# First stage as a planned order of steps, and the last two dense blocks of a chunk interleaved by pairs of channel tiles

## The chip, the cores and the metric

The kernel runs on one core of one Trainium2 chip. The metric is the device time of one execution in microseconds (us). Five engines run side by side, each with its own queue of instructions, taken in order: TensorE (PE: matrix products; its weight loads are listed as PEld), VectorE (DVE), ScalarE (ACT), GpSimd (POOL) and SyncE (SP), which here does little but issue DMAs. An instruction that waits for another engine holds up all that stands behind it on its own engine.

## What is computed

One layer of a streaming encoder on 4096 tokens of width 1024, in float32. Cut to what matters here:

```python
h = rms_norm(x, norm_g[layer])
proj = h @ w_in[layer]                       # 1024 -> 4648 columns
q, k, v, qi, ki, wi, z_a, u_b, z_b, gates = jnp.split(proj, SPLIT_POINTS, axis=-1)
q = apply_partial_rope(rms_norm(q, q_norm_g[layer]), cos_a, sin_a)
k = apply_partial_rope(rms_norm(k, k_norm_g[layer]), cos_a, sin_a)
...                                          # qi, ki turned alike
iscore = jnp.einsum('bqhs,bqh->bqs', jax.nn.relu(logits), wib)
_, idx = lax.top_k(iscore, k_sel)            # 256 keys of each query
a = dsa_attention(q, k, v, qi, ki, wi, k_sel) * jax.nn.silu(z_a)
b = multiscale_pool(u_b, pool_w[layer], pool_scale[layer]) * jax.nn.silu(z_b)
g = jax.nn.sigmoid(gates.reshape(B, S, N_BRANCHES, D_MODEL) + merge_bias[layer])
y = g[:, :, 0] * (a @ w_branch_a[layer]) + g[:, :, 1] * (b @ w_branch_b[layer])
x = x + y @ w_out[layer]
```

## The kernel before

Products of float32 are made of three products of halves: every operand is split into a high part (rounded to the PE's input format, written by ACT) and a low part (the rest, a subtraction), and high x high, high x low and low x high are summed in PSUM (`mm3`, L342). The work has four stages, one behind the other.

**First stage (`phase1`, L351).** For each of 32 tiles of 128 tokens: load x, its mean square (`stats`, L382), scale it, turn it 128 x 128 on PE with the halves split out of PSUM (`transp`, L391, two times four turns), project it with 1064 columns of `w_in` in three groups, q (512 columns), kv (256) and i (296) (`project`, L407), and then `evac` (L417): norms and rotation of q and k on ACT, DVE and POOL, the halves written to DRAM. `index_key` (L470) turns the index key of a tile into the resident array `kis`. The halves of h go to DRAM too (`hD`), for the dense products of the second stage. The order of the instructions is the order in which the code is written: L497 to L568 give a start by hand, and a loop in which tile t is projected while tile t + 2 is turned and the statistics of tile t + 3 are made. In the start, tiles 0 and 1 are projected 256 columns at a time as the split weights come in (`weights`, L476, whose raw tiles have two buffers); the angle tables (`tables`, L285) are made ahead of that on DVE. A PSUM buffer `pt` (two of them) takes the turned x and also the turned index key.

**Second stage (`phase_index`, L660).** The search of the 256 keys runs beside the dense products of the columns that are left. The order is made by a planner (`Plan`, L146): each step has an engine, a cost, a key (about a due time) and the steps it waits for; `run` plays them in order of keys with these costs and calls each step's function when it starts, which writes the instruction. So the order of each engine is fixed when the kernel is built, from the planner's costs, and the chip's own times decide only how long the engines wait for each other. The search: scores on PE (`ps`, L767), Relu on ACT (L770), the weighted sum on DVE (L772) into `ring`; then seven rounds of counting per group of query tiles (ACT `sg`, L857, and the update of the bound on DVE, L816 to L845), the 256th value (L885 to L897, `flag`) and the bias rows (L905). A count of the flags (L935) is read by all engines before the third stage.

The dense products (`dense`, L941): six sweeps of four or five blocks of 128 columns; each sweep goes over eight chunks of 512 tokens, and for each chunk over its blocks, each of 24 products of 512 columns into a PSUM buffer `pd` (three of them). The halves of h come from DRAM as eight tiles `h` per chunk (pairs of channel tiles, high and low, 512 KB each) into a ring of 12. A block ends in a sigmoid on ACT (`sgm`, L969, L1004, L1011), which frees `pd` or lets DVE free it.

**Third and fourth stage**: attention over the chosen keys, and the output products. The change doesn't touch their code.

Of the kernel before, what the change touches and what calls it, by code (L numbers as in the profile page):

```python
# [24 lines left out]
NB = S // P  # L25
# [83 lines left out]
WSP = 10000.0  # L109
HLD = 40.0  # L110
# [24 lines left out]
class Plan:  # L135
# [43 lines left out]
    def run(self, lat):  # L179
# [12 lines left out]
        while left:  # L192
# [16 lines left out]
            if start:  # L209
# [8 lines left out]
                busy[s.eng] = now + s.cost + (CHF if form.get(s.eng, 0) != s.form else 0.0)  # L218
# [17 lines left out]
            else:  # L236
                assert nxt is not None, "the plan has no step to go on with"
                now = nxt
        return now
# [13 lines left out]
class K:  # L253
# [6 lines left out]
    def consts(self):  # L260
        nc, cp, a = self.nc, self.cp, self.a
# [5 lines left out]
        ii = c1.tile([P, P], I32, name="ii")  # L267
        nc.gpsimd.iota(ii, pattern=[[1, P]], base=0, channel_multiplier=-1)
        self.ident = ci.tile([P, P], F32, name="ident")
        nc.vector.tensor_scalar(self.ident, ii, 0.0, None, op0=OP.is_equal)  # L270
        self.identr = cp.tile([P, P], F32R, name="identr")
        nc.scalar.activation(self.identr, self.ident, AF.Copy)
        self.kis = ci.tile([P, S], F32R, name="kis")
        self.wi = ci.tile([P, NB, 8], F32, name="wi")
        self.qn2 = ci.tile([P, NB, 9], F32, name="qn2")
        self.k31 = ci.tile([P, P], F32R, name="k31")
# [4 lines left out]
        nc.scalar.dma_start(self.cst, a["cst"])  # L281
        nc.scalar.dma_start(self.col, a["col"])
        self.gqk = c1.tile([P, 10, 64], F32, name="gqk")

    def tables(self, rp):  # L285

        nc, a = self.nc, self.a
        with self.tc.tile_pool(name="prep", reuse_waits="tile", bufs=1) as sp:
            pos_i = sp.tile([P, NB], I32, name="pos_i")
            nc.scalar.dma_start(pos_i, a["pos"])  # L290
            gq = sp.tile([P, 2, 64], F32, name="gq")
            nc.scalar.dma_start(gq[:, 0], bass.AP(tensor=a["q_norm_g"].tensor, offset=a["q_norm_g"].offset,
                                                  ap=[[0, P], [1, 64]]))
            nc.scalar.dma_start(gq[:, 1], bass.AP(tensor=a["k_norm_g"].tensor, offset=a["k_norm_g"].offset,
                                                  ap=[[0, P], [1, 64]]))
            nc.vector.tensor_scalar(self.gqk[:, 0:8], bc(gq[:, 0:1], [P, 8, 64]), 0.125, None, op0=OP.mult)
            nc.vector.tensor_copy(self.gqk[:, 8:10], bc(gq[:, 1:2], [P, 2, 64]))
            pos = sp.tile([P, NB], F32, name="pos")
            nc.vector.tensor_copy(pos, pos_i)

            sh = [P, NB, 12]
# [10 lines left out]
            for piece in TWO_PI[:3]:  # L312
                for m in (nh, nl):
                    nc.vector.scalar_tensor_tensor(ang, m, -piece, ang, op0=OP.mult, op1=OP.add)
# [1770 lines left out]
```

## Time and profile before

| | us |
|---|---|
| time, median of 3 runs (4126.26 to 4133.24) | 4131.97 |
| the profiled execution, its own time | 4129.07 |
| its span, first to last instruction | 4127.3 |
| PE busy in the span | 3975.5 (96%) |
| DVE busy | 3239.9 (78%) |
| ACT busy | 2254.5 (55%) |
| POOL busy | 2012.3 (49%) |

A busy PE is not a PE at its peak: its products overlap, and a row's length is longer than the distance to the next row. So the text below goes by the distance from start to start. "Idle before" is the time that an engine stood still just ahead of an instruction, and the engine behind the arrow is the one that ended the wait. In a row of the timeline the columns are start, length, engine, line, operation, what is written `<-` what is read, and count. Where the trace gives a clock (PEclk), it is the share of full speed that was granted to TensorE.

### The profile page before, as it was taken

The page shows a single profiled execution, that of the slowest core. Times are in us where ns is not written, and L with a number is a line of the kernel's source. Part 1 is how long each engine was busy: PE and PEld are TensorE (multiplying, and loading weights), DVE is VectorE, ACT ScalarE, POOL GpSimd, SP SyncE. Part 2 cuts the span into 40 slices and gives each one's busy share as a digit, 9 for nine tenths or more (in the row PEclk, how much of TensorE's full clock was granted, in tenths as well). Part 3 has the DMA queues.
Part 4 walks back from the last instruction along what each step waited for, and adds up shares of the span by engine and source line. Part 5 has one row for each costly group of instructions (what it writes and reads, how often), then busy time and mean ns, then how long its engine had stood idle before and what let it go on. Part 6 is the DMA issues. An engine that isn't in the chain of part 4 may idle for free.

```text
span 4127.3 us, 63967 instructions
## 1 busy us (share of the span) xinstructions
PE 3975.5 (96%) x22940; PEld 3030.1 (73%) x22941; DVE 3239.9 (78%) x6389; ACT 2254.5 (55%) x3163; POOL 2012.3 (49%) x1623
## 2 busy tenths in 40 slices
PE   7999999999999999999979999999999999999999
PEld 6888888787777777788756666666666666887887
DVE  5555688888888888777679999999999995556654
ACT  4444687777777877877545555555554543111221
POOL 3555412213213223010028889999999994334653
PEclk9999999999999999999979999999999999999999
DMA  7766645544446446566563443332222215887543
GB/s 232 272 237 231 201 168 179 181 165 166 169 164 204 145 153 203 209 230 213 203 150 73 78 75 66 59 62 54 56 54 43 47 25 165 282 256 237 189 158 123
DMA packets 515986, 637.36 MB, mean 154 GB/s; under 512 B 230608, under 2 KB 365392, under 8 KB 511696
## 3 DMA queue, kind: packets, MB, share of 16 engines
q1 hardware_dynamic: 487632, 608.18, 46.7%
q10 hardware_dynamic: 28032, 25.06, 2.7%
q8 instruction: 181, 2.97, 0.3%
q14 instruction: 141, 1.16, 0.1%
HBM read 409.48 MB, written 191.76 MB: 146 GB/s over the span
## 4 chain that ended last, share of the span: by engine, by line
PE 60%; DVE 15%; issue 7%; ACT 5%; POOL 5%; DMA 5%; SPq 1%; ACTq 0%; DVEq 0%; POOLq 0%
PE pv L1550 8%; PE p L2003 7%; PE st L1498 7%; PE p L1854 7%; PE pd L1061 7%; PE pd L1060 7%; PE pd L1062 6%; PE ps L767 4%; DVE jk L1439 4%; PE ps L1430 3%; DVE ring L772 2%; ACT sg L857 2%; DMA h<-hD 2%; POOL row L431 2%; DVE tt L1511 1%
## 5 line engine op out<-in xcount | busy, mean ns | idle before, releaser
L1529 POOL TENSOR_TENSOR acc<-acc,tt 128x1024 f32<-128x1024 f32 x388 | 928.0, 2392 | 67.2 <-ACT tt L1510 40.4
L1510 ACT ACTIVATE tt<-tt 128x1024 f32<-128x1024 f32 (+1 forms) x544 | 560.9, 1034 | 553.0 <-DVE tt L1511 520.0
L1061 PE MATMUL pd<-h,wgh 128*128 128x512 f32 x1792 | 706.3, 394 | 9.0 <-DMA h<-hD 8.5
L1060 PE MATMUL pd<-h,wgh 128*128 128x512 f32 x1792 | 711.0, 397 | 0.3 <-DMA h<-hD 0.3
L772 DVE SCALAR_TENSOR_TENSOR ring<-rl,wi,ring 128x1024 f32<-128x1024 f32 (+7 forms) x624 | 698.2, 1165 | 11.3 <-ACT rl L770 8.0
L1062 PE MATMUL pd<-h,wgl 128*128 128x512 f32 x1792 | 705.7, 394 | 0.0
L770 ACT ACTIVATE rl<-ps 128x1024 f32<-128x1024 f32 (+7 forms) x624 | 536.2, 887 | 182.2 <-DVE ring L772 62.1
L1511 DVE TENSOR_TENSOR tt<-st,bT 128x1024 f32<-128x1024 f32 (+1 forms) x504 | 600.5, 1193 | 12.1 <-PE st L1498 11.9
L1550 PE MATMUL pv<-tt,vv 128*64 128x256 f32 x4224 | 518.9, 387 | 2.5 <-ACT ov L1571 1.9
L857 ACT ACTIVATE sg<-ring,tk 128x2048 fp8e4<-128x2048 f32 (+9 forms) x322 | 485.1, 1508 | 63.5 <-DVE tk L845 34.0
L1439 DVE CUSTOM_DVE_ANT_1 jk<-ps,bias,mf 128x1024 bf16<-128x1024 f32 (+3 forms) x408 | 469.4, 1151 | 19.5 <-PE ps L1430 17.5
L1550 PEld LDWEIGHTS pv<-tt,vv 128*64 128x64 f32 x4224 | 287.1, 138 | 171.6 <-issue 38.0
L1061 PEld LDWEIGHTS pd<-h,wgh 128*128 128x128 f32 x1792 | 338.1, 189 | 83.2 <-DMA h<-hD 15.5
L1062 PEld LDWEIGHTS pd<-h,wgl 128*128 128x128 f32 x1792 | 337.9, 189 | 75.5
L1060 PEld LDWEIGHTS pd<-h,wgh 128*128 128x128 f32 x1792 | 337.9, 189 | 74.4 <-DMA h<-hD 0.7
L767 PE MATMUL ps<-kis,qT 128*128 128x512 f32 (+3 forms) x1136 | 343.9, 388 | 40.2 <-ACT rl L770 40.0
L1854 PE MATMUL p<-g,w 128*128 128x512 f32 x1488 | 345.5, 394 | 1.7 <-DVE g L1777 1.7
L1854 PEld LDWEIGHTS p<-g,w 128*128 128x128 f32 x1488 | 279.3, 188 | 67.7 <-DVE g L1777 2.1
L2003 PE MATMUL p<-w,g 128*128 128x512 f32 x1344 | 315.0, 397 | 3.7 <-ACT g L2007 3.7
L2003 PEld LDWEIGHTS p<-w,g 128*128 128x128 f32 x1344 | 254.4, 189 | 64.2 <-ACT g L2007 4.2
L1430 PE MATMUL ps<-kh,qh 64*128 64x512 f32 (+3 forms) x1320 | 264.9, 418 | 29.6 <-DVE mf L1439 26.8
L767 PEld LDWEIGHTS ps<-kis,qT 128*128 128x128 f32 x1136 | 207.1, 189 | 116.4 <-ACT rl L770 75.0
(333 smaller groups left out, 6756.2 us busy)
## 6 DMA issues: line engine op xcount, KB each, us to landing
h<-hD SPq DMA_DIRECT2D x384, 512.0 KB
g<-gD SPq DMA_DIRECT2D x80, 512.0 KB
hlD<-rhl SPq DMA_DIRECT2D x31, 1216.0 KB
gD<-sgm SPq DMA_DIRECT2D x128, 256.0 KB
q<-hlD SPq DMA_DIRECT2D x61, 512.0 KB
x<-x SPq DMA_DIRECT2D x32, 512.0 KB
hD<-hh SPq DMA_DIRECT2D x32, 512.0 KB
hD<-hl SPq DMA_DIRECT2D x32, 512.0 KB
```

Source lines behind the costliest of these rows:

```text
L767: pe.matmul(ps.t[:, s:e], t.t[:, h], self.kis[:, o + s:o + e], start=True, stop=True)
L772: prev[o] = pl.add("dve", 0.1 + n * 1.04e-3, k_, lambda rl=rl, o=o, n=n, h=h: v.scalar_tensor_tensor(acc[:, o:o + n], rl.t[:, :n], self.wi ...
L857: mine.append(pl.add("act", 0.28 + m * 0.834e-3, key, lambda sg=sg, o=o, m=m, e=e, j=j, b=b: act.activation(sg.t[:, o:o + m], where[b][:, ...
L1060: pe.matmul(out, wh.t[:, k], r1, start=(k == 0), stop=False)
L1061: pe.matmul(out, wh.t[:, k], r2, start=False, stop=False)
L1062: pe.matmul(out, wl.t[:, k], r1, start=False, stop=(k == KT - 1))
L1439: v.tensor_tensor_reduce(out=jk.t[:, :2 * (hi - lo) * P].rearrange("p (t n) -> p t n", t=2), in0=flat().rearrange("p (t n) -> p t n", t=2) ...
L1511: ad = last_ve[0] = pl.add("dve", 0.07 + 0.54 * n, key, lambda: v.tensor_tensor(tt.t[:, 0:n], s.t[:, 0:n], bc(bt.t[:, 2 * p:2 * p + n, Non ...
L1529: gp.tensor_tensor(acc.t, first, tt.t, op=OP.add)
L1550: pe.matmul(pv.t[64 * f:64 * f + 64], vv[:, k, 64 * g:64 * g + 64], T[u, p].t[:, k % 2, 2 * f:2 * f + 2], start=(k == 0), stop=(k == b))
L1854: pe.matmul(p.t, blk[i].t[:, k, ms], two(x[k // 2][j].t, F32R)[:, k % 2], start=(k == i == j == 0), stop=(k == 3 and i == 1))
L2003: pe.matmul(p.t, quarter(Q.t, x, F32R)[:, k], blk[y].t[:, k], start=(fresh and k == x == y == 0), stop=(k == 3 and x == 1), skip_group_che ...
```

## The change

There are two parts.

**The first stage becomes a plan.** The hand-written order is replaced by steps of the same `Plan` that orders the second stage. Its parts:

- `begin` (new): POOL clears a buffer and PE multiplies it 18 times, in nine steps, for nothing (`WARM`); the norm's gain is loaded as one row of 4 KB and spread to 128 partitions by two products with a row of ones, where before a DMA read it 128 times.
- `tables`: the same operations as single steps with keys of their own, behind the first projections; the small loads go through SP and not through ACT's queue.
- The weights are loaded by SP without waiting for buffers, each piece of 128 columns into a tile of its own, and tiles 0 and 1 are projected piece by piece (`piece`): nine pieces (eight of 128 columns, one of 40) of 3 x 8 products each, high x high first, then low h, then low w. The low parts of q's pieces 0 and 2 are made on POOL (`ON_POOL`).
- The Newton step of `rsqrt` is on DVE for tiles 0 and 1.
- In the loop, PE's order is tied down (each step waits for the one before): q, four turns, kv, four turns, i, index key. The index key is turned into the free columns of `mb` and not into `pt`. The evacuations, statistics and loads are placed by the planner, with a key of 12.45 us per tile.
- The weights of the first dense blocks are loaded and split inside the plan, and the second stage's plan starts from what the first one left on each engine (`left`, `late`). The index keys of tiles 30 and 31 are turned in the second stage.

**The last two blocks of a chunk are interleaved.** In `dense` the last two blocks of each chunk go over the pairs of channel tiles together: channel tiles 0 and 1 of one block, 0 and 1 of the other, 2 and 3 of one, and so on. A pair of `h` tiles is then last read earlier within the chunk.

From here on the names of before stand with their own line numbers; the same operations stand at other lines in the changed kernel. The diff, cut to its core:

```diff
+WARM = 9
+ON_POOL = {("q", 0), ("q", 2)}
...
+    def begin(self, pl, sp, xp, gn):
...
+        s0 = pl.add("pool", 0.6, -99, lambda: po.memset(w.t[:, 0:4].bitcast(F32), 0.0), use=[w])
...
+        def warm():
+            for _ in range(2):
+                pe.matmul(pt.t.rearrange("p h q -> p (h q)"), w.t[:, 0], w.t[:, 0:4].rearrange("p k n -> p (k n)"), start=True,
+                          stop=True)
+        for i in range(WARM):
+            s0 = pl.add("pe", 0.86 if i < 4 else 0.44, -50 + i, warm, [s0], use=[w, pt])
...
+            for f in range(2):
+                fs = slice(f * 512, f * 512 + 512)
+                pe.matmul(ma.t[:, fs], row, x.t[0:1, fs], start=True, stop=True)
...
+            def piece(t, key, j, at, prev):
...
+                for i, (x, w, after) in enumerate(((hh, wh, high + [hi]), (hl, wh, low), (hh, wl, [lo]))):
+                    def mm(i=i, x=x, w=w):
+                        for k in range(KT):
+                            pe.matmul(m.t[:, c + o:c + e], x.t[:, k], w[:, k, o:e], start=(i == k == 0), stop=(i == 2 and k == KT - 1))
+                    prev = pl.add("pe", 8 * 0.5e-3 * max(e - o, 64), at, mm, after + [prev], use=[m, hh, hl])
...
+            for t in range(2, NB):
+                if t + 2 < NB:
+                    load_x(t + 2, tp[t + 2] - 72)
+                    stats(t + 2, tp[t + 2] - 36)
...
+                prev = project(t, "q", prev)
+                if t + 2 < NB:
+                    prev = transp(t + 2, 0, tp[t] + 5.6, prev)
+                prev = kv = project(t, "kv", prev)
+                if t + 2 < NB:
+                    prev = transp(t + 2, 1, tp[t] + 8.6, prev)
+                prev = project(t, "i", prev)
...
+                if t > 2:
+                    prev = index_key(t - 2, M[t][1], 384, tp[t] + 11, prev)
+                late.append(evac(t, kv, prev, tp[t] + 8.5))
...
-                for m, (kind, i) in enumerate(mine):
-                    pd = new("pd")
+                pds = [new("pd") for _ in mine]
+                ends = {}
+                todo = [(m, k) for m in range(len(mine) - 2) for k in range(KT)]
+                todo += [(m, k) for k0 in range(0, KT, 2) for m in (len(mine) - 2, len(mine) - 1) for k in (k0, k0 + 1)]
+                for m, k in todo:
```

How it moves instructions, at the three places of which the prediction speaks. First the start of the first stage. On PE there stood at the front of the program, with `x` tile 0, `wqh`/`wql` the halves of q's weights and `hh`/`hl` those of the turned x:

```order
L398 MATMUL pt<-ident,x 128x128 x8
L347 MATMUL ma<-wqh,hh 128x256
L348 MATMUL ma<-wql,hh 128x256
L349 MATMUL ma<-wqh,hl 128x256
L347 MATMUL ma<-wqh,hh 128x256
L348 MATMUL ma<-wql,hh 128x256
```

Now there stands on PE (the 18 products for nothing write `pt_146`; tile 0 is `x_142`, tile 1 `x_166`):

```order
L301 MATMUL pt_146<-hh_138 128x512 x4
L311 MATMUL ma_154<-x_140,onerow 128x512 x2
L301 MATMUL pt_146<-hh_138 128x512 x14
L473 MATMUL pt_193<-ident,x_142 128x128 x4
L473 MATMUL pt_202<-ident,x_142 128x128 x4
L524 MATMUL ma_213<-wqh,hh_194 128x128 x8
L524 MATMUL ma_213<-wqh,hl_195 128x128 x8
L524 MATMUL ma_213<-wql,hh_194 128x128 x8
L524 MATMUL ma_213<-wqh,hh_194 128x128 x8
```

And on DVE, at the same place of the changed kernel (`h_111` is the raw second piece of q's weights, `hl_195` the low part of tile 0):

```order
L460 SCALAR_TENSOR_TENSOR x_142<-x_142,rs_159,gn 128x512 x2
L506 TENSOR_TENSOR wql<-h_111,wqh 128x8x128
L476 TENSOR_TENSOR hl_195<-pt_193,hh_194 128x512
L476 TENSOR_TENSOR hl_195<-pt_202,hh_194 128x512
L450 TENSOR_SCALAR rs_211<-rs_211 128x1
```

PE's products of 256 columns have become runs of eight products of 128 columns, and the low part of tile 0 stands behind that of q's second piece on DVE.

Second, the end of a tile in the loop, on PE, before (`rhk` is the index key of the tile two back):

```order
L347 MATMUL mb<-wih,hh 128x296
L348 MATMUL mb<-wil,hh 128x296
L349 MATMUL mb<-wih,hl 128x296
L341 MATMUL pt<-identr,rhk 128x128
L347 MATMUL ma<-wqh,hh 128x512
```

and now:

```order
L401 MATMUL mb_2427<-wih,hh_2067 128x296
L402 MATMUL mb_2427<-wil,hh_2067 128x296
L403 MATMUL mb_2427<-wih,hl_2068 128x296
L395 MATMUL mb_2427<-identr,rhk_2215 128x128
L401 MATMUL ma_2472<-wqh,hh_2223 128x512
```

The index key no longer takes a `pt` buffer, which DVE frees (L401), but columns of the tile's own `mb`.

Third, the end of the search on ACT: `sg` are the counting rounds of the last group (two query tiles, of 384 and 512 keys, one round is a pair of rows), `sgm` the sigmoids of the last dense blocks. Before:

```order
L857 ACTIVATE sg_20735,tk_19744<-ring,tk_19744 128x384
L857 ACTIVATE sg_20737,tk_19744<-ring,tk_19744 128x512
L1004 ACTIVATE sgm_20769<-pd_20682 128x512
L857 ACTIVATE sg_20774,tk_19744<-ring,tk_19744 128x384
L857 ACTIVATE sg_20794,tk_19744<-ring,tk_19744 128x512
L1004 ACTIVATE sgm_20824<-pd_20765 128x512
L1004 ACTIVATE sgm_20868<-pd_20820 128x512
L1004 ACTIVATE sgm_20894<-pd_20864 128x512
L1078 TENSOR_LOAD cnt
```

and now:

```order
L1140 ACTIVATE sgm_20989<-pd_20892 128x512
L993 ACTIVATE sg_20994,tk_20185<-ring,tk_20185 128x512
L1140 ACTIVATE sgm_20998<-pd_20908 128x512
L993 ACTIVATE sg_21024,tk_20185<-ring,tk_20185 128x384
L993 ACTIVATE sg_21026,tk_20185<-ring,tk_20185 128x512
L993 ACTIVATE sg_21050,tk_20185<-ring,tk_20185 128x384
L993 ACTIVATE sg_21052,tk_20185<-ring,tk_20185 128x512
L993 ACTIVATE sg_21075,tk_20185<-ring,tk_20185 128x384
L993 ACTIVATE sg_21077,tk_20185<-ring,tk_20185 128x512
L993 ACTIVATE sg_21099,tk_20185<-ring,tk_20185 128x384
L993 ACTIVATE sg_21107,tk_20185<-ring,tk_20185 128x512
L1220 TENSOR_LOAD cnt
```

Three sigmoids stood behind the last round; now four rounds stand behind the last sigmoid. Of the 5376 dense products 300 stood behind the last scores on PE (L767), and 180 do now. Behind the load of `cnt` the order of PE, DVE, ACT and POOL is the same in both kernels.

More of the change, by code (lines that the diff above doesn't have):

```diff
@@ L217, in run @@
                 s.fn()
-                busy[s.eng] = now + s.cost + (CHF if form.get(s.eng, 0) != s.form else 0.0)
+                s.end = busy[s.eng] = now + s.cost + (CHF if form.get(s.eng, 0) != s.form else 0.0)
                 form[s.eng] = s.form
@@ L238, in run @@
                 now = nxt
+        self.busy = busy
         return now
@@ new lines, in index_key, with hkt, tk @@
+            def index_key(t, out, o, key, prev):
+                hk, have = HK[t]
+                def hkt():
+                    return hk.t
+                def tk(out):
+                    return out.t[:, 0] if out.ring == "pt" else out.t[:, o:o + P]
+                s = pl.add("pe", 0.13, key, lambda: self.turn(tk(out), hkt()), [have, prev, self.have[1]], use=[out, hk])
+                pl.add("act", 0.27, key, lambda: act.activation(self.kis[:, t * P:(t + 1) * P], tk(out), AF.Copy), [s],
+                       use=[out])
+                return s
@@ new lines, in phase1 @@
+            load_x(0, -100)
+            stats(0, -30)
+            for f in range(2):
+                transp(0, f, -35 + f)
+            first = (("q", 0), ("q", 1), ("x", 1), ("q", 2), ("q", 3), ("x", 2), ("kv", 0), ("kv", 1), ("x", 3), ("i", 0), ("i", 1),
+                     ("i", 2))
+            for n, (kind, j) in enumerate(first):
+                if kind == "x":
+                    load_x(j, -90 + n)
+                else:
+                    weights(kind, j, -40 + n)
+            self.tables(pl, xp, 26.0)
@@ new lines, in phase1 @@
+            for t in range(1, 4):
+                stats(t, t * 2.0 - 30, [x[0] for x in turned[0]])
+            ends = {}
+            for f in range(2):
+                transp(1, f, -17 + f)
+            last = {0: None, 1: None}
+            for n, (key, j) in enumerate(x for x in first if x[0] != "x"):
+                for t in range(2):
+                    last[t] = piece(t, key, j, n + t * 2.5, last[t])
+                    if (key, j) == ("kv", 1):
+                        ends[t] = last[t]
+                if key == "kv":
+                    transp(2, j, n + 2.0)
+                elif key == "i" and j < 2:
+                    transp(3, j, n + 4.0)
@@ L582, in split @@
+            pl.run(LAT)
+            zero = pl.busy["pe"]
+            self.left = {e: max(0.05, pl.busy[e] - zero) for e in ("act", "dve", "pool", "dma")}
+            self.late = [max(0.1, max(s.end for s in late[t]) - zero) for t in (NB - 2, NB - 1)]
+        self.es1.close()
     def split(self, pool, src, shape, name, place=""):
@@ L681, in phase_index @@
         v.memset(self.flag, 0.0)
-        for _ in range(2):
-            self.split_w()
         pl.ring("qi", 1, lambda i: self.q30)
```

576 lines of the change are left out of this document (310 added, 266 removed).

## Prediction

> **What bounds the kernel now.** I first read the busy time by stretches, cut at PE's own marks: its first product (17.04), the first product of tile 2 in the loop (59.00), the end of the first stage (448.88), the last dense product (2064.10).
>
> ```profile
> core 0: us, PE busy (x) PEld busy (x) DVE busy (x) ACT busy (x) POOL busy (x), PEclk, DMA share, GB/s
> 0.00:17.04 17.04, 0.00 (x1) 0.02 (x2) 6.22 (x17) 7.57 (x13) 2.39 (x10) 1.00 0.87 275
> 17.04:59.00 41.96, 34.42 (x224) 32.81 (x225) 28.72 (x52) 21.96 (x39) 10.03 (x30) 0.92 0.64 187
> 59.00:448.88 389.88, 381.94 (x2416) 342.02 (x2414) 196.39 (x408) 165.71 (x431) 192.88 (x524) 1.00 0.71 247
> 448.88:2064.10 1615.22, 1561.43 (x6856) 1247.51 (x6854) 1324.68 (x3532) 1225.92 (x1635) 322.18 (x306) 0.99 0.53 183
> 2064.10:4127.30 2063.20, 1997.67 (x13449) 1407.73 (x13448) 1683.86 (x2382) 833.32 (x1045) 1484.78 (x755) 0.98 0.43 113
> ```
>
> PE is the bound: from 59.00 on it stands still 7.9 us in the first stage and 53.8 in the second. A change of order that leaves the products alone can take away these waits and the start, no more. The last stretch holds nothing of the change. Next PE's waits, first in the loop of the first stage, then in the second stage, with the waits of ACT for dense blocks:
>
> ```profile
> PE pt L341 <- DVE hl L401: 6.9, 23, 2.2
> PE ps L767 <- ACT rl L770: 40.0, 39, 3.4
> PE pd L1061 <- DMA h<-hD: 8.5, 9, 2.1
> ACT sgm L1011 <- PE pd L1062: 62.6, 56, 4.8
> ACT sgm L1004 <- PE pd L1062: 33.9, 14, 5.2
> ```
>
> (total, times, longest). The loop's wait is the index key's: it needs a `pt` that DVE hasn't emptied. The distance from tile to tile shows its whole price:
>
> ```profile
> 100.45 0.47 PE L347 MATMUL ma<-wqh,hh 128*128 128x512 f32 x1
> 400.12:412.72 12.60, 12.60 (x83) 11.47 (x82) 6.91 (x15) 4.67 (x13) 6.59 (x18) 1.00 0.60 224
> 425.32:437.12 11.80, 11.80 (x75) 10.72 (x74) 4.23 (x8) 4.69 (x10) 6.09 (x14) 1.00 1.03 289
> ```
>
> A tile without a wait takes 12.60 us (11.80 for tiles 30 and 31, beside which nothing is turned). The 30 tiles of the loop took 389.9; without waits 28 x 12.60 + 2 x 11.80 = 376.4. So 13.5 us are waits of the loop.
>
> **The start.** PE's first product waits 17 us, and what it multiplies by comes like this:
>
> ```profile
> 17.04 1.97 PE L398 MATMUL pt<-ident,x 128*128 128x128 f32 x8 [17.04 <-DVE x L389]
> 5.40 1.06 ACT L386 ACTIVATE sq<-x 128x1024 bf16<-128x1024 f32 x1 [1.59 <-DMA x<-x]
> 8.44 1.06 ACT L490 ACTIVATE wqh<-wraw 128x1024 fp32r<-128x1024 f32 x1 [1.89 <-DMA wraw<-w_in]
> 10.73 1.06 ACT L490 ACTIVATE wqh<-wraw 128x1024 fp32r<-128x1024 f32 x1
> 13.31 1.20 DVE L491 TENSOR_TENSOR wql<-wraw,wqh 128x1024 fp32r<-128x1024 f32 x1
> 22.61 0.68 DVE L401 TENSOR_TENSOR hl<-pt,hh 128x512 fp32r<-128x512 f32 x1
> L1030 POOL TENSOR_TENSOR wgl<-wraw,wgh 128x1024 fp32r<-128x1024 f32 x24 | 64.7, 2697 | 139.3 <-ACT wgh L1029 139.3
> ```
>
> x is there at 5.40, the first pieces of q at 8.44 and by 10.73. In the changed kernel's DVE queue the low part of the second piece stands ahead of that of tile 0: 10.73 + 1.06 (ACT) + 1.20 + 0.68 = 13.7 before PE's second run of eight can start, and from then on everything is there or comes ahead of need. The low part of the first piece on POOL (2.70 by its row) ends at about 12.3, in time. The 18 products for nothing and the spread of the gain lie before that: from about 1 us, 18 to 20 products of 512 columns at 0.43 (half clock, row below) are 9 us; they cost nothing up to 13.7, and 2 to 4 us if the spread is slower than its form. The tables on DVE (some 12 us) move behind the first projections, where DVE is busy 196 of 390 us.
>
> What is left is 424 products of 128 columns (9 pieces x 2 tiles x 24, less 8), six times four turns. No row has such a product in a long run. The nearest:
>
> ```profile
> 64.59 0.60 PE L398 MATMUL pt<-ident,x 128*128 128x128 f32 x4
> 64.95 0.37 PE L347 MATMUL ma<-wkvh,hh 128*128 128x256 f32 x1
> 65.38 0.28 PE L347 MATMUL ma<-wkvh,hh 128*128 128x256 f32 x1
> 65.50 0.28 PE L348 MATMUL ma<-wkvl,hh 128*128 128x256 f32 x1
> ```
>
> Four turns of 128 columns start 0.09 apart (64.59 to 64.95), products of 256 columns 0.12. If only columns counted, 128 would be 0.059; if the weight load sets the distance, it is at most 0.12. I take 0.09, the row of that shape: 424 x 0.09 + 6 x 0.36 + 1.5 for odd waits = 41.9, so tile 2 starts at 13.7 + 41.9 = 55.6 and not at 59.0: **-3.4 us**, with ends at 13.7 + 25.0 + 3.7 = 42.4 (-17) and 13.7 + 50.9 + 3.7 = 68.3 (+9). [...]
>
> **The loop.** The order on PE is the same but for the buffer of the index key, so the wait of 23 keys for DVE's `hl` goes. What is late next: DVE, ACT and POOL have 6.9, 4.7 and 6.6 us of work in a tile of 12.60, x is loaded four tiles ahead, and the statistics are due three tiles ahead of use, so nothing comes near. The eight `h` loads (512 KB each) that stood at tiles 20 to 26 stand on SP among the stores of the first ten tiles; at 247 GB/s the loop's own 3 MB a tile leave room, and no PE wait of the loop is for a DMA. I leave 1 us of waits: **-12.5**; ends -13.5 and 0 (rival below).
>
> **The handover to the second stage.**
>
> ```profile
> 448.76 0.22 PE L341 MATMUL pt<-identr,rhk 128*128 128x128 f32 x1
> 451.10 0.28 PE L341 MATMUL pt<-identr,rhk 128*128 128x128 f32 x1 [2.12 <-DVE rhk L459]
> 451.68 0.63 PE L1061 MATMUL pd<-h,wgh 128*128 128x512 f32 x1
> 448.88:455.00 6.12, 4.00 (x13) 3.10 (x12) 3.54 (x8) 3.38 (x10) 2.52 (x7) 0.72 0.36 135
> ```
>
> PE waits 2.1 us for tile 30's key and then runs at half clock (0.72 on average over 6.1 us), which costs 1.7 us more. Now three dense products stand ahead of that key, and 33 more (8 us) ahead of tile 31's, whose evacuation is short of that by little. I take -4 and 1 for a wait at the second key: **-3** (ends -4 and +1). [...]
>
> **The second stage.** Its products are the same, so only waits count; 51.7 of the 53.8 us are left after the handover.
>
> Interleaving frees the first pair of `h` tiles after 12 of the two blocks' 48 products instead of after 30, the second after 24 instead of 36 and the third after 36 instead of 42: the first 18 products, some 4 us, earlier, and the next chunk's loads go out earlier by that; of the 8.5 us of waits for `h` I take **-6** (ends 0 and -8.5).
>
> 120 dense products (28 us at 0.233) move from behind the last scores to ahead of them. There PE waits 40.0 us for Relu; products put into such gaps cost nothing. Which of them fall into gaps no row tells: between 0 and -28, and I take **-12**, since about a third of the second stage's time lies in stretches where PE never waits.
>
> The price stands at the stage's end:
>
> ```profile
> L767 PE MATMUL ps<-kis,qT x68: 222/393/497, 1900.9 to 1987.4; 128*128 128x512 f32 x46, 128*128 128x384 f32 x14, 128*128 128x128 f32 x8
> 2038.45 0.61 ACT L857 ACTIVATE sg<-ring,tk 128x384 fp8e4<-128x384 f32 x1
> 2042.35 0.61 ACT L857 ACTIVATE sg<-ring,tk 128x384 fp8e4<-128x384 f32 x1 [2.36 <-DVE tk L845]
> 2046.65 0.61 ACT L857 ACTIVATE sg<-ring,tk 128x384 fp8e4<-128x384 f32 x1
> 2054.93 0.16 DVE L897 TENSOR_TENSOR flag<-sel 128x1 f32<-128x1 f32 x1
> 2056.29 0.22 PE L935 MATMUL pd<-flag,one 128*1 128x32 f32 x2
> 2063.87 0.40 PE L1062 MATMUL pd<-h,wgl 128*128 128x512 f32 x1
> 2065.11 0.87 PE L341 MATMUL st<-identr,k 128*128 128x128 f32 x8 [0.84 <-ACTq L1079]
> ```
>
> Before, the search ended first (flag at 2054.93), under dense products that ran to 2064.1, and PE went on 1.24 us after its last one. Now four rounds stand on ACT behind the last sigmoid, which waits for the last dense product. A free round takes 3.90 (2038.45 to 2042.35); from the last round's start to the last flag it took 8.3, of which 3 were a wait for a dense block, so 5; count and branch about 2.5. So PE stands still for 2 (sigmoid, bound) + 3 x 3.90 + 5 + 2.5 = 21.2 us: **+20** (ends +16, if the rounds overlap better, and +24).
>
> **Sum**: -3.4 - 12.5 - 3 - 6 - 12 + 20 = -16.9 us on an execution of 4129.07, which lies 2.9 below the median of 4131.97. For the median: 4131.97 - 16.9 = 4115.
>
> **The rivals.**
>
> *Columns alone count in the start.* If products of 128 columns start 0.059 apart, the start gains 17 and not 3.4: 4115 - 13.6 = 4101. For it: 256 columns take half of 512 (0.12 to 0.23). Against: four turns at 0.09. Chance 0.13.
>
> *The loop keeps its pace.* The planner's costs decide the order, and one of them is short of its row: POOL's product with the gains (L431) takes 2.54 where the plan has 1.7. If an evacuation so comes to stand ahead of what frees PE each tile, the 12.5 us are lost: 4127.5, within what a measurement can't tell from no change (0.2%, 8.3 us). Against: half of each engine's time is free. With it goes the case that no moved product falls into a gap (4127). Together 0.22.
>
> *ACT is stopped at the paired sigmoids* (the other side). Place: ACT's queue at the end of each of the 48 chunks. Both blocks of a pair now end 1.4 us apart, and ACT, which stops for PE in 70 of these sigmoids already, 1.1 us at a time (62.6 in 56), holds up Relu and counting behind them. One such stop more per chunk is 48 x 1.1 = 53 us for the search, which now ends last; with two thirds of it reaching the end, +35: 4150. It decides from 17 us that get through, 0.35 us a chunk. For it: ACT is busy 1226 of 1615 us. Against: PE has dense products ready meanwhile, and the number of sigmoids is the same. Chance 0.13.
>
> **Numbers.** Forecast 0.52. Faster (below 4123.7): the forecast, the first rival, less a little of the forecast's upper end: 0.64. Within 0.2%: 0.23. Slower: 0.13. The range runs from 4092 (the fast start and half of the gaps together) to 4140, which takes in the second rival and the smaller half of the third.
>
> **What would show it.** In the changed profile: tile 2's first q product at 55 to 56 (42 and 68 are the ends); tiles 12.6 us apart, no wait of L341 for `hl`; the last of the first stage near 432; no row at half clock at the handover; fewer waits for `h`; after the last dense product PE idle 20 us, with four pairs of `sg` on ACT in it. I am wrong if tiles stay at 13.0, if the idle end is under 10 us, or if PE's waits for Relu grow past 60 us.

## The result and the profile after

The changed kernel takes 4157.75 us (median of 5 runs, 4154.23 to 4158.58); before takes 4131.97 (5 runs, 4126.26 to 4136.77). The ratio is 1.0058, 95% interval 1.0046 to 1.0070: slower by 0.6%, where 4115 was forecast and the range ended at 4140. Timed again beside the experiments the ratio was the same (`e16_changed` below). One execution of `e14_seqbal` below took 9164.65 us, in a slow state, and its ratio leaves it out.

The profiled execution has a span of 4156.8 us against 4127.3, and a mean granted clock of 0.981 against 0.988. Busy time by stretches of the changed kernel, cut at PE's own marks: its first turn of x (12.72), the first product of tile 2 (71.49), the last key of the first stage (451.11), the end of the last dense product (2070.00), the start of attention (2095.00):

```profile
core 0: us, PE busy (x) PEld busy (x) DVE busy (x) ACT busy (x) POOL busy (x), PEclk, DMA share, GB/s
0.00:12.72 12.72, 10.69 (x23) 5.99 (x24) 5.62 (x15) 4.95 (x9) 3.38 (x8) 1.00 0.96 268
12.72:71.49 58.77, 58.61 (x464) 58.06 (x465) 30.09 (x52) 19.73 (x37) 8.40 (x20) 0.89 0.47 138
71.49:451.11 379.62, 379.62 (x2416) 346.33 (x2414) 212.88 (x425) 178.47 (x444) 210.07 (x536) 1.00 0.75 256
451.11:2070.00 1618.89, 1563.53 (x6853) 1257.81 (x6852) 1310.53 (x3421) 1215.15 (x1612) 321.10 (x300) 0.99 0.54 182
2070.00:2095.00 25.00, 0.27 (x4) 0.14 (x3) 14.29 (x108) 8.17 (x19) 0.40 (x2) 0.61 0.20 67
2095.00:4156.80 2061.80, 2000.90 (x13448) 1409.75 (x13448) 1683.09 (x2380) 831.20 (x1043) 1483.88 (x753) 0.98 0.43 112
```

Set against the same stretches of before:

| stretch | before | after | difference | forecast |
|---|---|---|---|---|
| to tile 2's first product | 59.00 | 71.49 | +12.5 | -3.4 |
| loop of the first stage | 389.88 | 379.62 | -10.3 | -12.5 |
| from there to the last dense product | 1615.22 | 1618.89 | +3.7 | -21 (handover -3, `h` -6, Relu -12) |
| idle end, to attention | 1.01 | 25.00 | +24.0 | +20 |
| attention and output | 2062.19 | 2061.80 | -0.4 | 0 |
| sum | 4127.3 | 4156.8 | +29.5 | -16.9 |

The two profiled executions differ by 29.5 us, the medians by 25.8. So the loop's gain and the idle end came about as forecast. The start lost where it was to gain, and the second stage gave nothing where it was to give 21. PE's waits in the changed kernel (total, times, longest):

```profile
PE ps L903 <- ACT rl L906: 47.4, 35, 4.7
...
PE pd L1071 <- DVE flag L1033: 19.4, 1, 19.4
...
PE pd L1200 <- issue: 3.4, 1, 3.4
...
PE pd L402 <- POOL pl L1126: 3.2, 6, 0.8
```

The rows of L341 for `hl` and of the dense products for `h` are gone. The waits for Relu, which were to shrink from 40.0, are 47.4.

**The start.** PE's rows between 53 and 76 us (start, length, engine, line, operation, output `<-` inputs, count):

```profile
53.60 1.01 PE L524 MATMUL mb<-wih,hh 128*128 128x40 f32 x8
...
57.17 1.08 PE L524 MATMUL mb<-wih,hl 128*128 128x128 f32 x8
58.06 1.90 PE L524 MATMUL mb<-wil,hh 128*128 128x128 f32 x8
59.76 1.91 PE L524 MATMUL mb<-wih,hh 128*128 128x128 f32 x8
...
71.49 0.78 PE L401 MATMUL ma<-wqh,hh 128*128 128x512 f32 x1
...
74.63 0.63 PE L402 MATMUL ma<-wql,hh 128*128 128x512 f32 x1
...
75.33 0.39 PE L401 MATMUL ma<-wqh,hh 128*128 128x512 f32 x1
```

Two things are to be seen. Eight products start 0.86 to 0.93 us after the eight before them, 0.11 apart, whether they have 128 columns or 40: the forecast had 0.09. And at 58.06 the rows get nearly twice as long (1.90 in place of 1.08) and stay so until 75, though PE isn't idle for a moment (busy in all of the 22.00 us from 53.00 to 75.00): the clock was halved for 17 us (0.50 from 58.06 to 75.00).

**The handover.** The last key of the first stage on PE, DVE's row that reads the accumulator `ma` of tile 31 last, and the first dense product:

```profile
450.89 0.22 PE L395 MATMUL mb<-identr,rhk 128*128 128x128 f32 x1
453.56 0.82 DVE L557 TENSOR_TENSOR row<-ma,ss 128x640 f32<-128x640 f32 x1 [1.19 <-POOL ss L390]
454.49 0.76 PE L1200 MATMUL pd<-h,wgh 128*128 128x512 f32 x1 [3.37 <-issue]
455.05 0.63 PE L1201 MATMUL pd<-h,wgh 128*128 128x512 f32 x1
```

"issue" says that the profile found no releaser. But DVE's row ends at 454.38, and PE goes on 0.11 later; `e4_bank` shows that this is the wait. Behind it the clock is halved (0.63 for a product that takes 0.39).

**The end of the search.** The last scores, and the rows at the end of the stage:

```profile
L903 PE MATMUL ps<-kis,qT x1136: 220/394/797, 471.7 to 2028.3; 128*128 128x512 f32 x176, 128*128 128x128 f32 x6, 128*128 128x256 f32 x5, 128*128 128x384 f32 x3
```

```profile
2069.39 0.39 PE L1201 MATMUL pd<-h,wgh 128*128 128x512 f32 x1
2069.62 0.39 PE L1202 MATMUL pd<-h,wgl 128*128 128x512 f32 x1
2070.04 0.60 ACT L1140 ACTIVATE sgm<-pd 128x512 f32<-128x512 f32 x1
2089.08 0.16 DVE L1033 TENSOR_TENSOR flag<-sel 128x1 f32<-128x1 f32 x1
2089.38 0.26 PE L1071 MATMUL pd<-flag,one 128*1 128x32 f32 x2 [19.38 <-DVE flag L1033]
2095.00 0.47 PE L395 MATMUL st<-identr,k 128*128 128x128 f32 x2 [5.35 <-ACT ones L1315]
```

The last scores come at 2028.3, where they came at 1987.4 before. From there to the last flag it takes 60.8 us (67.5 before); the 180 dense products that are left last 42, at 0.23 apart. So PE stands still for 19.4 us until the flag, and 5.6 more for count and branch.

### The profile page after: what moved, and what is told of

It reads as the page before. It is cut to its first block, busy times and chain, and to the rows that moved or that the text cites. A ratio compares the mean times of both kernels' runs of the same rounds, so it can differ in the third digit from the quotient of the medians.

```text
span 4156.8 us, 64440 instructions
## 1 busy us (share of the span) xinstructions
PE 4013.6 (97%) x23202; PEld 3078.1 (74%) x23203; DVE 3256.5 (78%) x6399; ACT 2257.7 (54%) x3163; POOL 2027.2 (49%) x1618
## 5 line engine op out<-in xcount | busy, mean ns | idle before, releaser
L1581 DVE CUSTOM_DVE_ANT_1 jk<-ps,bias,mf 128x1024 bf16<-128x1024 f32 (+3 forms) x408 | 469.6, 1151 | 20.9 <-PE ps L1572 19.2
L903 PE MATMUL ps<-kis,qT 128*128 128x512 f32 (+3 forms) x1136 | 345.1, 390 | 47.9 <-ACT rl L906 47.4
```

What stands on the lines that cost most here:

```text
L903: pe.matmul(ps.t[:, s:e], t.t[:, h], self.kis[:, o + s:o + e], start=True, stop=True)
L1581: v.tensor_tensor_reduce(out=jk.t[:, :2 * (hi - lo) * P].rearrange("p (t n) -> p t n", t=2), in0=flat().rearrange("p (t n) -> p t n", t=2) ...
```

## The experiments

Ratios are to the kernel before on the same chip in the same job, with 95% intervals; "idle end" is the time from the end of the last dense product to attention.

| run | what | median us | ratio | last scores, us after the first stage's last product of i | idle end |
|---|---|---|---|---|---|
| before | | 4127.6 to 4132.9 | 1 | 1538 | 0.8 |
| e16_changed | the changed kernel | 4158.9 | 1.0058 (1.0040 to 1.0076) | 1579 | 24.8 |
| e1_interleave | before + interleaving | 4145.2 | 1.0048 (1.0029 to 1.0066) | 1564 | 26.6 |
| e2_first | planned first stage alone | 4132.2 | 1.0010 (0.9998 to 1.0022) | 1537 | 1.1 |
| e3_wide | no product of 40 columns | 4133.8 | 1.0014 (1.0004 to 1.0024) | 1566 | 25.2 |
| e4_bank | `pd` elsewhere in PSUM | 4155.4 | 1.0064 (1.0044 to 1.0084) | 1574 | 24.6 |
| e6_seq | e2 + e3 + e4 | 4115.3 | 0.9956 (0.9942 to 0.9971) | 1537 | 1.2 |
| e7_cost | dense step at 0.656 | 4157.5 | 1.0056 (1.0039 to 1.0073) | 1556 | 4.7 |
| e8_all | e3 + e4 + e7 | 4137.7 | 1.0012 (0.9999 to 1.0026) | 1544 | 4.8 |
| e9_cover | e3 + e4, step at 0.6375 | 4102.8 | 0.9941 (0.9921 to 0.9961) | 1530 | 3.9 |
| e10_late | e3 + e4, interleaving in the last two sweeps alone | 4102.9 | 0.9945 (0.9924 to 0.9967) | 1532 | 8.1 |
| e11_early | e3 + e4, interleaving in the first four sweeps alone | 4131.2 | 1.0004 (0.9993 to 1.0014) | 1556 | 7.2 |
| e12_bias | e9, bias stores on POOL | 4115.8 | 0.9968 (0.9957 to 0.9979) | 1541 | 3.7 |
| e13_balance | changed, step at 0.6375 | 4122.4 | 0.9983 (0.9973 to 0.9993) | 1532 | 3.6 |
| e14_seqbal | e6, step at 0.6375 | 4133.1 | 1.0000 (0.9990 to 1.0010) | 1532 | 1.2 |
| e15_oldbal | e1, step at 0.6375 | 4112.9 | 0.9957 (0.9940 to 0.9973) | 1533 | 3.7 |

**Each part alone.** `e1_interleave` puts the new `todo` list into `dense` of the kernel before:

```diff
-                for m, (kind, i) in enumerate(mine):
-                    pd = new("pd")
...
+                todo = [(m, k) for m in range(len(mine) - 2) for k in range(KT)]
+                todo += [(m, k) for k0 in range(0, KT, 2) for m in (len(mine) - 2, len(mine) - 1) for k in (k0, k0 + 1)]
```

> The kernel before with the interleaved last two blocks alone; its first stage is the hand-written one. Theory: the interleaving is what puts the last scores behind more dense products (195 stand behind them here, 300 before, 180 in the changed kernel), so the search ends last and PE stands still at the stage's end; the whole loss of the second stage is here: last flag 25 to 35 us later than 2054.9, PE idle 20 to 25 us behind the last dense product, no wait for h, median 4132 + 20 to 30, so 4152 to 4162. Rival (the planned first stage makes it, by the later start that it hands to the second plan): no idle end, h waits gone, 4122 to 4132.

`e2_first` is the changed kernel with the same lines turned back:

> The changed kernel with the dense blocks one behind the other as before: the planned first stage alone. Theory: the start stays 12.5 us late (tile 2 at 71.5), the loop saves 10.3, the handover costs 1; the second stage as before (300 dense products behind the last scores, search hidden, h waits of 8 to 9 us): 4132 + 2 to 5, so 4134 to 4137. Rival (the idle end belongs to the planned first stage): the search ends last here too, PE idle over 15 us at the stage's end, 4150 to 4160.

With the interleaving alone there is an idle end of 26.6 us, without it 1.1. PE's longest wait of e1:

```profile
PE pd L935 <- DVE flag L897: 21.4, 1, 21.4
```

So the idle end belongs to the interleaving, and the rival falls. The planned first stage costs what its stretches said: 72.26 - 59.00 = +13.3 in the start, 378.87 - 389.92 = -11.1 in the loop; its ratio can't be told from 1. The median of e1 was 7 us below what was expected: its stretch from the first to the last dense product took 1607.5 us and before's 1613.1, since the waits for `h` are gone.

**Narrow products and the clock.** `e3_wide` makes one product of 168 columns out of the last two of i in tiles 0 and 1:

```diff
+                his, los = [hi], [lo]
+                if (key, j) == ("i", 1):
+                    _, e, hi, lo = pieces[key][2]
+                    his, los = his + [hi], los + [lo]
```

> The changed kernel; in its start the products of the last 128 and 40 columns of i are one product of 168, so that no product of 40 columns is left; everything else as it was. Theory (the clock halves because the 24 products of 40 columns from 53.6 on use PE too little): no half clock in the start; tile 2 starts at 71.5 less 8.5 for the clock, less 48 products of 40 columns at 0.111 (5.3), plus 48 times the difference of 168 to 128 columns (under 1): 57 to 59, and 4157.8 - 13 = 4143 to 4146. Rival (44 us of products of 128 columns, half of PE's time unused, halve it in the end): half clock comes all the same within some us of 58, tile 2 at 62 to 66, 4149 to 4153.

Its start, with the clock in the third column from the right, and PE's rows at the end of it:

```profile
12.72:59.76 47.04, 46.88 (x416) 46.33 (x417) 30.16 (x50) 19.29 (x37) 8.73 (x20) 1.00 0.58 172
```

```profile
56.27 1.08 PE L528 MATMUL mb<-wih,hh 128*128 128x168 f32 x8
57.18 1.06 PE L528 MATMUL mb<-wih,hl 128*128 128x168 f32 x8
58.07 1.06 PE L528 MATMUL mb<-wil,hh 128*128 128x168 f32 x8
58.97 1.04 PE L473 MATMUL pt<-ident,x 128*128 128x128 f32 x8
59.76 0.48 PE L401 MATMUL ma<-wqh,hh 128*128 128x512 f32 x1
```

Full clock throughout, and tile 2 starts at 59.76 and not at 71.49. Eight products of 168 columns take as long as eight of 128 or 40 (0.89 to 0.91 us from start to start, against 0.86 to 0.93), so the 48 narrow ones cost 48 x 0.111 = 5.3 us besides the clock. The first stage is 13.5 us shorter (437.66 to 451.11), as expected. The time fell by more: by 27.4 us between the two profiled executions and by 0.44%, 18 us, between the ratios. The order behind the first stage is the same in both; what is left, 5 to 14 us, lies mostly in the second stage (1603.6 against 1615.5 us from the first to the last dense product). Of these 11.9 us 7.6 lie in PE's busy time (1563.5 to 1555.9, for the same products) and 4.3 in its waits for Relu (47.4 to 43.1). By the granted clock the stage lost 13.8 us here and 22.8 in the changed kernel (the sum is explained at the end), which fits the busy time. Why the clock was halved less often in the same order is not settled.

That no idle time is needed was then tried by itself. `e5_narrow` puts runs of extra products behind the projections of six tiles of e3's loop:

```diff
+PROBE = {8: (40, 24), 12: (40, 48), 16: (128, 48), 20: (64, 48), 24: (16, 48), 28: (88, 48)}
...
+                    for k in range(count):
+                        pe.matmul(m.t[:, 296:296 + n] if n <= 64 else m.t[:, 384:384 + n], hh.t[:, k % KT], wh[:, k % KT, 0:n],
+                                  start=True, stop=True)
```

> The kernel with the start of e3 (no product of 40 columns in the program), and behind the projections of six tiles of the loop a run of extra products into unused columns, whose results nothing reads: 24 of 40 columns at tile 8, 48 of 40 at tile 12, 48 of 128 at tile 16, 48 of 64 at tile 20, 48 of 16 at tile 24, 48 of 88 at tile 28. PE has no idle time there. Theory (few columns per product halve the clock, not idle time alone): products start 0.111 apart at every width, the clock halves within 5 us of the runs of 40 and of 16 columns and not at 128; 64 and 88 show where the limit lies. Rival (the halving in the start was made by something else there, DMA or the many weights loaded anew): full clock at all six.

The stretches from the starts of the runs (148.25, 203.00, 263.71, 319.69, 377.11, 437.86) on, cut where the clock changes; after the length comes PE's busy time, the clock is third from the right:

```profile
148.25:150.86 2.61, 2.61 (x27) 2.61 (x25) 2.61 (x4) 1.31 (x4) 0.02 (x1) 1.00 0.83 331
150.86:154.28 3.42, 3.42 (x11) 2.74 (x11) 1.96 (x5) 0.68 (x3) 0.99 (x5) 0.50 0.98 293
203.00:205.48 2.48, 2.48 (x25) 2.48 (x24) 0.82 (x1) 0.00 (x0) 1.54 (x2) 1.00 0.97 332
205.48:215.72 10.24, 10.24 (x39) 9.27 (x39) 2.22 (x7) 3.65 (x10) 4.69 (x14) 0.50 0.21 74
263.71:274.00 10.29, 10.29 (x72) 9.40 (x71) 3.18 (x8) 3.65 (x10) 5.66 (x15) 1.00 0.45 157
319.69:324.94 5.25, 5.25 (x50) 5.25 (x48) 0.82 (x1) 0.00 (x0) 3.35 (x6) 1.00 0.74 257
324.94:328.36 3.42, 3.42 (x11) 2.75 (x11) 0.68 (x3) 2.73 (x9) 1.73 (x7) 0.50 0.08 32
379.56:389.80 10.24, 10.24 (x39) 9.27 (x39) 2.15 (x7) 3.65 (x10) 4.74 (x14) 0.50 0.20 72
437.86:447.00 9.14, 9.14 (x67) 8.47 (x66) 2.50 (x5) 2.52 (x7) 4.94 (x11) 1.00 0.26 93
```

PE is busy in all of it. The runs of 40, 64 and 16 columns (first, second, fourth and fifth) halve the clock 2.5 to 5.3 us after their start, for 3.4 or 10.2 us; those of 128 and 88 columns (third and sixth) don't. The rival falls. (Its time, of one run, is 4179.6 us, with the extra products and the half clock in it.)

**The handover.** `e4_bank` lays the first `pd` over a `pt`:

```diff
-        for name, i in (("ps", 0), ("pd", 0), ("pd", 1), ("pd", 2), ("pt", 0), ("ps", 1)):
+        for name, i in (("pd", 0), ("ps", 0), ("pd", 1), ("pd", 2), ("pt", 0), ("ps", 1)):
```

> The changed kernel; in the second stage the first buffer pd changes its place in PSUM with the first ps, so that it no longer lies over the accumulator ma of tile 31 but over a pt. Theory (the first dense product waited 3.4 us for the last reader of tile 31's ma, the scaling of q and k on DVE that ended at 454.4): the first dense product comes right behind the last index key at 451.1 with no wait, no half clock behind it, the second stage 3.4 + 1 us earlier: 4157.8 - 4 to -5, so 4152 to 4154. Rival (it waited for something else, the weights or h): the wait of 3.4 us stays, 4157 to 4158.

The 6.1 us behind the last key, of e4:

```profile
452.69:458.80 6.11, 6.11 (x29) 4.97 (x28) 4.60 (x10) 2.75 (x11) 4.44 (x15) 1.00 0.38 154
```

and of the changed kernel:

```profile
451.11:457.22 6.11, 2.74 (x8) 2.17 (x8) 4.61 (x10) 2.86 (x11) 4.36 (x15) 0.74 0.38 154
```

29 products in place of 8, full clock in place of 0.74: the wait was for `ma` of tile 31. The median didn't show the 4 to 5 us (1.0064 here, 1.0058 without, the intervals cover each other): in the profiled execution the start was 2 us longer, since the clock was halved for longer (20.5 us; in the profile of e16 it was 23.9, so the start differs by some us from execution to execution).

**The parts put together.** `e6_seq` is e2 with both edits:

> The planned first stage with e3's start and e4's place of pd, and the dense blocks one behind the other as before. Theory (the parts add up): e2's 4132 less 13 for the start (no half clock, fewer products) less 4 for the handover: 4113 to 4118, idle end about 1 us, waits for h 8 to 10 us; that is faster than before. Rival (what is won ahead of the second stage is given back by its waits): 4124 to 4132.

0.9956: the parts add up (4132 - 17 = 4115), and the planned first stage is worth 0.4% once its start and handover are mended.

**The plan's balance.** The planner takes a dense step of three products for 0.625 us; the rows at 2069 have 3 x 0.23 = 0.69. `e7_cost` raises this:

```diff
-                        prev = pl.add("pe", 5.0 / KT, t, mm, [l0, l1, have, prev], use=[pd, wh, wl, h0, h1])
-                        t += unit / KT
+                        prev = pl.add("pe", 5.25 / KT, t, mm, [l0, l1, have, prev], use=[pd, wh, wl, h0, h1])
+                        t += unit / KT
```

with `unit` at 5.29 in place of 5.04.

> The changed kernel with the planner's cost of a dense step (three products) raised from 0.625 to 0.656 and the due times with it; the trace has 0.68 to 0.70. 393 dense products stand behind the last scores (180 in the changed kernel), so the order of the second stage is another. Theory (the plan takes PE to be faster than it is, and so puts more dense products ahead of the scores than fit beside the search; put behind, they hide the search's tail and lose nothing): idle end 0 to 2 us, PE's waits for Relu not above 50 us, 4157.8 - 22 to -28, so 4130 to 4136. Rival (the moved products did fill gaps, and the gaps come back): idle end gone, but waits for Relu up by 12 us or more, 4142 to 4150.

The idle end shrank to 4.7 us, as both have it, and the time stayed, above both ranges. The named waits for Relu rose by 4.8 us and not by 12:

```profile
PE ps L903 <- ACT rl L906: 52.2, 42, 3.9
```

The stretch from the first dense product to the last is 27.7 us longer than in the changed kernel (1643.2 against 1615.5): 11.9 of it lie in PE's waits (4.8 for Relu, 3.6 for the sigmoids), and 15.8 in its busy time. That PE, with 393 dense products held back behind the last scores, had too few to put beside the search fits this, but no run shows it by itself. `e8_all`, the same with e3 and e4, came out on the side of its rival:

> e7 with e3's start and e4's place of pd: the changed kernel with its interleaving kept and the three losses taken away. Theory: e7 less 13 for the start less 4 for the handover, no waits for h: 4113 to 4119, faster than before. Rival (the interleaving's own order costs more on ACT and DVE than the h waits it saves): over 4124.

1.0012, no better than e3. `e9_cover` takes the value in between (5.1, `unit` 5.14), which leaves 300 products behind the last scores as before:

> e8 with the planner's cost of a dense step at 0.6375 in place of 0.656: the whole interleaving kept, e3's start, e4's place of pd, and 300 dense products behind the last scores, as many as in the kernel before (180 in the changed kernel, 393 in e8). Theory A (all that the interleaving costs is the search's tail without cover: 67 us from the last scores to the last flag, 300 products are 69): idle end 0 to 4 us, no h waits, so e6 (0.9956 of before) less 8 to 12: 0.993 to 0.994 of before. Theory B (the interleaving also costs inside: SP stands 257 to 269 us at the loads of h instead of 67, the stores of bias rows stand behind them, and DVE's waits for those are 32 to 40 us instead of 21 to 22): idle end small, but scores that come 10 to 20 us later against the dense products, 0.996 to 1.000 of before.

0.9941, theory A. From the first dense product to attention e9 takes 1603.3 us and e6 1615.4. e6 waits 12.3 us for `h` and e9 1.4; the waits for Relu fell too (35.9 to 28.4), and the idle end and the waits for `pl` took 5.5 back. So with this cost the interleaving is worth about those waits. Three runs on its inside, made in the same job:

> e3's start and e4's place of pd, interleaving in the last two sweeps alone (the two with four gate blocks a chunk); 294 dense products stand behind the last scores. Theory A (tail alone): covered, h waits only of the first four sweeps, 0.994 to 0.996 of before. Theory B (SP at the h loads, by the chunk): a third of the loss of e9 against e6 (0.9956), 0.995 to 0.997.

> e3's start and e4's place of pd, interleaving in the first four sweeps alone (those with pool blocks); 270 dense products stand behind the last scores, 62 us, so some 5 of the tail's 67 us are not covered. Theory A: idle end 3 to 8 us, h waits nearly gone: 0.994 to 0.997 of before. Theory B: two thirds of the loss inside, idle end besides: 0.997 to 1.001.

> e9 with the stores of the bias rows issued from POOL's queue in place of SP's, where they no longer stand behind loads of h; the order of PE's, ACT's and DVE's instructions is the same. Theory B (the queue): DVE's waits for the bias stores fall from over 30 us to under 15, the scores come earlier and PE's waits for Relu fall: 5 to 15 us faster than e9. Theory A or any other cause inside (ACT, the buffers pd): DVE's waits fall, and the time stays within 4 us of e9, or is longer because POOL now stops for DVE.

`e10_late` came out as theory A has it (0.9945), but for an idle end of 8.1 us; its interval takes in theory B as well. `e11_early` came out in theory B's range (1.0004, where A had at most 0.997): the interleaving of the first four sweeps is where the plan with 0.625 goes wrong. `e12_bias` was 13 us slower than e9, and DVE's waits for the bias stores, which the edit was to lower, rose from 26.0 to 36.6 us, so it doesn't show what the queue of SP costs. Against theory B speaks e9 itself: it lies below B's range (0.996 to 1.000), with waits for the bias stores of 26.0 us where B had 32 to 40. What the interleaving of the first four sweeps costs inside the plan with 0.625 is left open.

What was left was the cost alone. `e13_balance` is the changed kernel with this cost, and the due times that go with it:

```diff
-                        prev = pl.add("pe", 5.0 / KT, t, mm, [l0, l1, have, prev], use=[pd, wh, wl, h0, h1])
+                        prev = pl.add("pe", 5.1 / KT, t, mm, [l0, l1, have, prev], use=[pd, wh, wl, h0, h1])
...
-        unit = 5.04
+        unit = 5.14
```

> The changed kernel with one number changed: the planner's cost of a dense step 0.6375 in place of 0.625 (due times with it), nothing else. 300 dense products stand behind the last scores in place of 180. Theory (the plan's balance is the whole loss of the second stage): idle end 1 to 5 us in place of 25, the 30 queries' flags 20 to 30 us earlier, waits for Relu not above 45 us: ratio to before 0.5 to 0.7% lower than the changed kernel's in the same job, 4130 to 4138. Rival (e9's gain came from the start and the place of pd, which let the second stage's waits fall otherwise): above 4145.

> The changed kernel itself, in the same job, so that e13 is compared on one chip. Both theories: half clock from 57 to 59 to 75, idle end 24 to 26 us, 1.005 to 1.007 of before; the clock lost in the second stage, 22.8 us in its first profile, anywhere from 12 to 24.

36 us between the two on one chip: 1.0058 to 0.9983, from one number, and more than was expected (4122.4 us, where the range began at 4130). Its second stage, its waits and its last scores:

```profile
452.67:2053.52 1600.85, 1558.99 (x6855) 1246.85 (x6854) 1314.91 (x3527) 1221.14 (x1628) 328.30 (x300) 0.99 0.53 184
2053.52:2057.13 3.61, 0.00 (x0) 0.03 (x1) 0.69 (x1) 0.60 (x1) 0.00 (x0) 0.80 0.78 203
```

```profile
PE ps L903 <- ACT rl L906: 30.0, 32, 3.4
```

The stage is 18 us shorter ahead of the last dense product too, the waits for Relu are 30.0 us in place of 47.4, and by the granted clock 8.8 us were lost in place of 22.8. How far the dense products run ahead can be counted on PE: ahead of the 600th of the 1136 score products stand 2718 of them in before, 2793 in the changed kernel, 2709 in e13. `e15_oldbal` and `e14_seqbal` turn it round:

> e1 (the kernel before with the interleaving alone) with the same 0.6375; 300 dense products behind the last scores in place of 195. Theory (the interleaving with a balanced plan saves the waits for h and loses nothing): idle end 1 to 5 us, before less 8 to 12: 0.997 to 0.998. Rival (it needs the planned first stage's hand-over): 1.002 or more.

> e6 (start of e3, place of pd, blocks one behind the other) with the same 0.6375. 378 dense products behind the last scores, where the tail needs 290. Theory (0.625 was right for this order because loads of h held the dense products back; a higher cost holds back products that filled waits): waits for Relu up, 4116 to 4135, not faster than e6 at 0.9956. Rival (the cost itself is simply better): 4100 to 4108, as e9 without its interleaving.

The kernel before with the interleaving goes from 1.0048 to 0.9957 by the same number; the order without interleaving goes the other way, from 0.9956 at 0.625 to 1.0000. So a cost isn't good by itself: it balances a given order, and the interleaving shifted the balance. The time of e14 came as its theory has it, but not by the waits for Relu, which were to rise and went from 35.9 to 34.6 us: of the 13.6 us by which its stretch of dense products is longer than e6's, 8.5 lie in PE's busy time (1562.6 to 1571.1).

## Why the prediction was wrong

**Start: -3.4 forecast, +12.5 measured.** Two terms failed. The spacing of products of 128 columns was taken from a row of four turns (0.09); it is 0.111, at 40 columns as at 168, near the end of the range that was named for it (0.12). That is 424 x 0.021 = 9 us. The row was misread: 0.36 us lie between it and the row behind, but the product behind follows the last turn after 0.03 already, and the turns themselves are 0.11 apart. With one turn and with all four the row of before is this long, 0.33 us more for three more turns:

```profile
64.59 0.27 PE L398 MATMUL pt<-ident,x 128*128 128x128 f32 x1
64.59 0.60 PE L398 MATMUL pt<-ident,x 128*128 128x128 f32 x4
```

The other term wasn't in the sum: the clock at half from 58.06 on, (71.49 - 58.06) / 2 = 6.7 us ahead of tile 2 and 1.8 behind. Two small misses cancelled: the second run of eight started at 15.28 and not at 13.7, and the 1.5 us for odd waits weren't needed. The forecast knew the halving behind idle time alone (the wait of 2.12 us at 451.10).

**Loop: -12.5 forecast, -10.3 measured.** The mechanism was right: the wait for `hl` is gone and nothing else came in its place; 1.8 of the missing 2.2 us are the end of the half clock, and in e3 the loop takes 377.9, 12.0 less than before.

**Handover: -3 forecast, a wait of 3.4 in place of 2.1.** The wait for the key went, and a new one took its place, by an address. As the planner gives out buffers, the products that spread the gain take the first `ma`, and so tile 0 gets the second and tile 31 the first, over which `pd` comes to lie. The order of instructions, from which the forecast argued, doesn't show addresses.

**`h`: -6 forecast, -8.5 measured,** all of the row.

**Relu: -12 forecast, +7.4 measured.** This is the step that failed most: "products put into such gaps cost nothing", with a third to a half of the 120 moved products in gaps. In the order that the plan made they stood ahead of scores that were due. The last scores came 39 us later (1577 against 1538), and the 120 products at 0.23 are 28 of these: nothing was won in gaps. That case stood in the prediction as a part of the second rival, at 4127. The 11th of the 30 flags came at 928 us after the first stage in before and at 962 in the changed kernel, the last at 1606 and 1638: the search had fallen back by 34 us by the middle of the stage and stayed so. The idle end and the missing gain are the same thing, seen at two places; the forecast priced the first and counted the moved products as a gain besides. Moving them is a gain only as far as the search keeps ahead; e7 and e14 show that holding more of them back than was balanced costs as much, though not by Relu's waits alone. Nor did the sum have a term for the clock inside the stage, which lost 22.8 us against 9.0 in before.

**Idle end: +20 forecast, +24 measured.** The mechanism was right: rounds on ACT behind the last sigmoid, with PE idle; the flag was there 19.2 us after the last dense product, and count and branch took 5.8 (2.5 forecast).

**The third rival named 4150,** near the result, and its mechanism is refuted: ACT's waits for dense blocks fell. The sigmoids of the gates and of z waited 62.6 + 33.9 = 96.5 us in before (the rows of L1011 and L1004 in the prediction), and now:

```profile
ACT sgm L1147 <- PE pd L1202: 41.5, 50, 2.6
ACT sgm L1140 <- PE pd L1202: 16.7, 13, 4.7
```

that is 58.2. A time near the measured one is no evidence for the story that came with it.

What stays open: which scores in the middle of the stage the plan with 0.625 puts too late and why the first four sweeps make it so (e11), by what e14 lost, and why the clock was halved less in e3's second stage than in the changed kernel's, in the same order.

## What to carry to other kernels

When an edit frees a buffer earlier inside a planned order, the planner's costs have to be balanced again before the edit is judged: here the same change was worth +0.6% or -0.2% by one number, the cost of a step, that stood 9% below its row, and neither of the two values that were tried on both orders was good for both. What a product costs in a run of short ones is to be taken from a run of that shape (here 0.111, where four turns had been read as 0.09), and pieces as narrow as 40 columns are better joined to their neighbour (in e3 this made the start 11.7 us shorter). Where one stage's buffers lie over the last one's, look which address the first instruction takes.

## What the runs showed of the hardware

- The clock of TensorE was halved not only behind idle time. In e5 PE had no idle time, and runs of 48 products of 16 or 40 columns, 0.11 apart, brought it to 0.50 for 10.2 us, 24 of 40 columns for 3.4, 48 of 64 columns for 3.4; at 88 and 128 columns it stayed at 1.00.
- Half clock came behind single waits inside the second stage as well. In the changed kernel 9 of 10 waits of 2 us or more were followed by half clock, in before 5 of 8; the shortest that was is 1.90 us, the longest that wasn't 3.23. One of them, with products of 512 columns that take 0.63 in place of 0.39:

```profile
1536.40 1.22 PE L903 MATMUL ps<-kis,qT 128*128 128x512 f32 x2 [2.54 <-ACT rl L906]
1537.41 0.63 PE L1200 MATMUL pd<-h,wgh 128*128 128x512 f32 x1
...
1539.44 0.40 PE L1201 MATMUL pd<-h,wgh 128*128 128x512 f32 x1
```

  Summing (1 - clock) x length over stretches of 20 us gives 22.8 us for the changed kernel's second stage and 9.0 for before's. How much of these 13.8 us the stage lost isn't shown: PE's busy time there rose by 2.1 us only (1561.43 to 1563.53), and its short waits, which a row's length of 0.39 at a distance of 0.23 covers, changed with the order as well. In the same order e3, with 13.8 in place of 22.8, was 11.9 us shorter.
- Products with a fresh weight load each started 0.111 us apart at 40 and 128 columns (the changed kernel) and at 168 (e3), about 0.11 at 16 and 64 (e5) and in the turns of 128 columns, and 0.213 apart at half clock, at 40 columns as at 128 (59.76 to 61.47 and 65.61 to 67.31 in the changed kernel, eight each).
